# Seven block products in place of eight for the first matrix of each FFN, and the adaLN rows spread over both matrices

## Chip, cores and metric

One NeuronCore of a Trainium2 chip runs the whole program. The metric is the device time of one execution in microseconds; the kernel before has a median of 2449.19 us over 3 runs (2449.11 to 2454.41).

## The reference

Two sequences (128 context tokens, 512 sample tokens) go through two layers with shared weights. A layer has three sublayers: an FFN, a mixing block and a second FFN, each between a modulated norm and a gated residual.

```python
def modulate(h, mod, j):
    return h * (1 + mod[:, j + 1][:, None, :]) + mod[:, j][:, None, :]

def swiglu(h, w1, w2):
    g, u = jnp.split(h @ w1, 2, axis=-1)
    return (jax.nn.silu(g) * u) @ w2

def ffn_half(x, mod, j, g_pre, g_post, w1, w2):
    h = modulate(rms_norm(x, g_pre), mod, j)
    return x + 0.5 * mod[:, j + 2][:, None, :] * rms_norm(swiglu(h, w1, w2), g_post)
```

D_MODEL is 1024, D_FF 2816, everything in float32. The adaLN rows `mod` (nine vectors of 1024 per layer, for the sample and for the context) are products of a conditioning vector with w_mod (1024 x 9216 per layer).

## The kernel before

The 640 tokens are five tiles of 128: the A tiles 0 and 1 (256 columns), and the B tiles 2, 3 (sample) and 4 (context), 384 columns. A sublayer's input is kept transposed, features on partitions, as two float32r parts (hi and lo) of A (`h0hi`, `h0lo`) and of B (`h1hi`, `h1lo`). Every weight tile (128x512, 256 KB) is fetched by SP into one of five `raw` tiles, and split: ScalarE writes `whi` (L269), VectorE `wlo` = raw - whi (L271; GpSimd takes a share of these at stage starts). Eight split pairs are held, so weights are split up to five units ahead of use (`prefetch`, `unit`). A product is three float32r matmuls (L309): hi x hi, hi x lo, lo x hi.

An FFN sublayer (stages 0, 2, 3 and 5 of six) runs its first matrix in 22 slices f of 128 of d_ff. For each f the gate part and the up part are summed over eight k tiles: per f 4 weight tiles, 48 matmuls of A and 48 of B. For the first f of a stage (7, 5, 5, 7: `N_AONLY`) A runs alone while the boundary of the B tiles (residual, norm, modulation, transposes, splits: `bnd_steps`) is still being computed; these weights are then fetched once more for B alone; the rest run for A and B together. Then `act` = silu(gate) * up (L524, L534). The second matrix makes two passes over w2: `ffn2(l, i, 0)` for A, and `ffn2(l, i, 1)` for B beside A's boundary (`second_pass`).

The adaLN rows for later sublayers (`ada`) are made beside the f that run for A and B: VectorE accumulates 1024 columns over eight chunks for two sequences (16 instructions at L377 per row), TensorE reduces over partitions (L386), and the row is parked in DRAM. There are 16 such rows: 6 in stage 0, 6 in stage 2, 3 in stage 3 and 1 in stage 5. Matmuls and work beside them are interleaved by `run` with a rate; the tile framework then fixes each engine's order, and every engine works through its own order without overtaking, and so does SP's queue of transfers.

Of the kernel before, what the change touches and what calls it, by code (L numbers as in the profile page):

```python
# [15 lines left out]
P = 128  # L16
D = 1024
# [21 lines left out]
KEEP_F, KEEP_C = 2, 4  # L39
# [9 lines left out]
# schedule of each sublayer: skews between the tiles of a boundary, Pool share, matmul units ahead  # L49
# [92 lines left out]
class Builder:  # L142
    def __init__(self, ctx, tc, a, n_stage=6):
# [6 lines left out]
        self.rawp = pool("raw", 5)  # L150
        self.wp = pool("wsp", 8)
# [47 lines left out]
    def plan(self):  # L199
        a = self.a  # L200

        def ffn(l, i):
            def f1(f):
                for part in range(2):
                    for half in range(2):
                        c0 = part * FF + f * P
                        src = a["ffn_w1"][l, i, 512 * half:512 * half + 512, c0:c0 + P]
                        self.units.append((("w1", l, i, f, part, half), [(slice(0, P), src.rearrange("(k p) f -> p k f", p=P))]))
            na = N_AONLY[3 * l + 2 * i]
            for f in range(na):  # L210
                f1(f)
            for f in range(max(0, na - KEEP_F)):
                f1(f)
            for f in range(na, NF):
                f1(f)
# [30 lines left out]
    def _dma(self, i):  # L246
# [9 lines left out]

    def prefetch(self, upto):
        n = len(self.units)
        upto = min(upto, n - 1)
# [1002 lines left out]
```

## Time and profile before

| what | value |
|---|---|
| median of 3 runs | 2449.19 us |
| span of the profiled execution | 2446.1 us |
| lowest run, so what lies around the span | 2449.11 us, 3.0 us |
| TensorE busy | 2393.9 us, 98% |
| VectorE / ScalarE / GpSimd busy | 59% / 39% / 15% |
| DMA | 360.06 MB, mean 147 GB/s |

The page does not print the profiled execution's own device time; the span runs from its first to its last instruction. PE is TensorE, DVE VectorE, ACT ScalarE, POOL GpSimd, SP the queue that issues transfers. Consecutive instructions of an engine overlap at their ends, so the distance of two starts in a full queue is shorter than the duration of one.

### The profile page before, as it was taken

The page shows a single profiled execution, that of the slowest core. Times are in us where ns is not written, and L with a number is a line of the kernel's source. Part 1 is how long each engine was busy: PE and PEld are TensorE (multiplying, and loading weights), DVE is VectorE, ACT ScalarE, POOL GpSimd, SP SyncE. Part 2 cuts the span into 40 slices and gives each one's busy share as a digit, 9 for nine tenths or more (in the row PEclk, how much of TensorE's full clock was granted, in tenths as well). Part 3 has the DMA queues.
Part 4 walks back from the last instruction along what each step waited for, and adds up shares of the span by engine and source line. Part 5 has one row for each costly group of instructions (what it writes and reads, how often), then busy time and mean ns, then how long its engine had stood idle before and what let it go on. Part 6 is the DMA issues. An engine that isn't in the chain of part 4 may idle for free.

```text
span 2446.1 us, 37268 instructions
## 1 busy us (share of the span) xinstructions
PE 2393.9 (98%) x13892; PEld 2139.2 (87%) x13892; DVE 1444.2 (59%) x2162; ACT 956.4 (39%) x1982; POOL 365.9 (15%) x432
## 2 busy tenths in 40 slices
PE   8999999999999999999999999999998999999998
PEld 6999998877778999988889999988787899999887
DVE  6568766675776577746565642364758654422454
ACT  5422225455665222225443222354555553222443
POOL 2000000133434000001040000010634450000000
PEclk9999999999999999999999999999999999999999
DMA  9356655452235566635465632454522344422542
GB/s 295 111 179 228 213 189 165 146 171 89 65 104 151 162 215 219 192 122 165 137 181 155 197 110 75 129 168 130 159 86 82 116 143 139 140 76 74 166 154 90
DMA packets 332043, 360.06 MB, mean 147 GB/s; under 512 B 22019, under 2 KB 241411, under 8 KB 331862
## 3 DMA queue, kind: packets, MB, share of 16 engines
q1 hardware_dynamic: 328262, 344.59, 45.4%
q10 hardware_dynamic: 3600, 13.11, 1.4%
q8 instruction: 108, 1.77, 0.3%
q14 instruction: 73, 0.60, 0.1%
HBM read 341.50 MB, written 16.12 MB: 146 GB/s over the span
## 4 chain that ended last, share of the span: by engine, by line
PE 88%; DVE 4%; POOL 3%; issue 2%; ACT 1%; SPq 1%; DMA 0%; DVEq 0%; POOLq 0%; ACTq 0%
PE PS L309 85%; PE PS L386 1%; POOL tmp L459 1%; POOL wlo L271 1%; DVE ast L899 1%; PE PS L466 1%; PE PS L922 1%; DVE tl L305 1%; DVE wlo L271 0%; ACT pt L905 0%; DVE h1lo L305 0%; POOL r L316 0%; SPq L253 0%; PE PS L1042 0%; SPq L989 0%
## 5 line engine op out<-in xcount | busy, mean ns | idle before, releaser
L269 ACT ACTIVATE whi<-raw 128x512 fp32r<-128x512 f32 x864 | 541.3, 629 | 1093.4 <-PE PS L309 999.0
L271 DVE TENSOR_TENSOR wlo<-raw,whi 128x512 fp32r<-128x512 f32 x810 | 596.7, 740 | 580.0 <-ACT whi L269 555.5
L309 PE MATMUL PS<-h1hi,wlo 128*128 128x384 f32 (+1 forms) x1408 | 477.9, 339 | 0.0
L309 PE MATMUL PS<-h1lo,whi 128*128 128x384 f32 (+1 forms) x1408 | 477.0, 339 | 0.0
L309 PE MATMUL PS<-h1hi,whi 128*128 128x384 f32 (+1 forms) x1408 | 475.2, 337 | 0.0
L309 PE MATMUL PS<-h0hi,whi 128*128 128x256 f32 x1408 | 400.4, 285 | 8.3 <-DVE act L534 8.3
L309 PE MATMUL PS<-h0hi,wlo 128*128 128x256 f32 x1408 | 399.6, 285 | 0.0
L309 PE MATMUL PS<-h0lo,whi 128*128 128x256 f32 x1408 | 397.6, 283 | 0.0
L309 PE MATMUL PS<-whi,ahi 128*128 128x512 f32 x920 | 355.4, 394 | 0.0
L309 PE MATMUL PS<-wlo,ahi 128*128 128x512 f32 x880 | 348.3, 396 | 0.0
L309 PE MATMUL PS<-whi,alo 128*128 128x512 f32 x840 | 331.5, 397 | 0.0
L377 DVE SCALAR_TENSOR_TENSOR acc<-wmt,ccs,acc 128x1024 f32<-128x1024 f32 x224 | 278.4, 1281 | 26.9 <-DMA wmt<-in_w_mod 26.5
L309 PEld LDWEIGHTS PS<-h0hi,whi 128*128 128x128 f32 x1408 | 267.0, 190 | 26.5 <-issue 11.7
L309 PEld LDWEIGHTS PS<-h0hi,wlo 128*128 128x128 f32 x1408 | 266.3, 189 | 9.3 <-issue 8.4
L309 PEld LDWEIGHTS PS<-h0lo,whi 128*128 128x128 f32 x1408 | 267.4, 190 | 4.4 <-issue 4.2
L309 PEld LDWEIGHTS PS<-h1lo,whi 128*128 128x128 f32 x1408 | 265.2, 188 | 4.2 <-issue 4.2
L309 PEld LDWEIGHTS PS<-h1hi,wlo 128*128 128x128 f32 x1408 | 265.7, 189 | 1.7 <-issue 1.7
L309 PEld LDWEIGHTS PS<-h1hi,whi 128*128 128x128 f32 x1408 | 265.8, 189 | 0.0
L309 PEld LDWEIGHTS PS<-whi,ahi 128*128 128x128 f32 x920 | 173.6, 189 | 39.2
L315 POOL TENSOR_SCALAR v<-ss 128x1 f32<-128x1 f32 x60 | 24.6, 410 | 1175.4 <-ACT mk L437 1132.6
L309 PEld LDWEIGHTS PS<-wlo,ahi 128*128 128x128 f32 x880 | 166.0, 189 | 38.6
L309 PEld LDWEIGHTS PS<-whi,alo 128*128 128x128 f32 x840 | 158.6, 189 | 34.3
(200 smaller groups left out, 2722.1 us busy)
## 6 DMA issues: line engine op xcount, KB each, us to landing
raw<-in_ffn_w SPq DMA_DIRECT2D x736, 256.0 KB
wmt<-in_w_mod SPq DMA_DIRECT2D x136, 512.0 KB
raw<-in_w_in SPq DMA_DIRECT2D x80, 256.0 KB
xd<-x ACTq DMA_DIRECT2D x25, 512.0 KB
x<-xd SPq DMA_DIRECT2D x25, 512.0 KB
raw<-in_w_out SPq DMA_DIRECT2D x64, 128.0 KB
mdG<-rowG SPq DMA_DIRECT2D x12, 512.0 KB
mdS<-rowS SPq DMA_DIRECT2D x10, 512.0 KB
```

Of the source, the lines that this page charges most:

```text
L269: self.nc.scalar.activation(hi, r, AF.Copy)
L271: eng.tensor_tensor(lo, r, hi.bitcast(F32), ALU.subtract)
L305: i1 = (eng or self.nc.vector).tensor_tensor(lo, src, hi.bitcast(F32), ALU.subtract)
L309: self.nc.tensor.matmul(out, w, m, start=start, stop=stop)
L315: self.nc.gpsimd.tensor_scalar(v, ss, add, EPS, ALU.add, ALU.add)
L377: nc.vector.scalar_tensor_tensor(accs[s], w, self.cc[:, s, k:k + 1], prev, ALU.mult, ALU.add)
L386: nc.tensor.matmul(ps[32 * q:32 * q + 32, :], self.ones[:, 0:32], accs[q // 2][:, 512 * (q % 2):512 * (q % 2) + 512], start=True, stop=Tru ...
L459: nc.gpsimd.tensor_tensor(tmp[:, hs], tmp[:, hs], self.md["T", st][:, hs], ALU.add)
L466: nc.tensor.transpose(ps[:, P * k:P * k + P], tmp[:, 512 * h + P * k:512 * h + P * k + P], self.ident)
L899: nc.vector.tensor_reduce(mx, S, AX.X, ALU.max)
L922: nc.tensor.transpose(ps[:, w * c + P * j:w * c + P * j + P], pt[:, n * j + P * (c0 + c):n * j + P * (c0 + c) + P], self.ident)
```

## The change

Write X for one FFN's normed input, X1 for the A tiles and X2 for the two B tiles of x_sample, each cut into the two halves of its 1024 features, and B11, B21 (gate part, two halves of the features) and B12, B22 (up part) for the four weight tiles of an f. The four outputs (gate and up of X1 and of X2) are eight block products; Winograd's form of Strassen's scheme makes them from seven, of sums and differences of blocks. The context tile has no partner and keeps its four block products, which ride along as 128 more columns.

- First part (`ffn1_first`): for all 22 f, A times B11 and A times B21, 24 matmuls of 256 columns each f. The first product is copied into the B activation tile, their sum is A's gate.
- Second part (`ffn1_rest`): per f five products with the weights T2 = B22 - B11', B11' = B12 - B11, B22, B12' = B12 - B22 and B21' = B21 - T2, 12 matmuls each, one of 256 and four of 384 columns (386 in stage 0). Seven VectorE additions and two copies of ScalarE take them out of PSUM, then two silu and two products.
- The four subtractions of weight tiles (`combine`) are three on VectorE and the fourth, B12', on GpSimd. All four raw tiles of an f must be there; all blocks are fetched anew for the second part, so B11 and B21 come twice: 112 raw tiles more than before.
- The B boundary forms the differences of input blocks (`S1`, `SZ`, and B's first half replaced).
- Three adaLN rows of stage 0 and two of stage 2 run beside the second part, at a rate of 0.5; four in stage 0, four in stage 2 and three in stage 3 run beside the second matrix at 0.8; stage 5 has none.

```diff
-N_AONLY = (7, 0, 5, 5, 0, 7)
-ADA_RATE = 0.65
+ADA_ROWS = {0: (((0, "GST"),), ((1, "GST"), (2, "G"))), 2: (((2, "ST"),), ((3, "GST"), (4, "G"))), 3: ((), ((4, "ST"), (5, "G"))), 5: ((), ())}
+ADA_RATES = (0.5, 0.8)
+Q_POOL = (3,)
...
+            for f in range(NF):
+                for half in range(2):
+                    self.units.append((("w1", l, i, f, half), w1(l, i, f, 0, half)))
+            for f in range(NF):
+                for n, blk in enumerate((None, (0, 0), (1, 1), (1, 0), (0, 1))):
+                    self.units.append((("wq", l, i, f, n), w1(l, i, f, *blk) if blk else []))
...
+    def combine(self, i):
+
+        t2, b11, b22, b12, b21 = (self.raws[i + j] for j in range(5))
+        for j, (o, x, y) in enumerate(((b11, b12, b11), (t2, b22, b11), (b21, b21, t2), (b12, b12, b22))):
+            eng = self.nc.gpsimd if j in Q_POOL else self.nc.vector
+            eng.tensor_tensor(o, x, y, ALU.subtract)
...
+            m6 = yield from prod(0, SZ, 0, W, lo4)
+            nc.scalar.activation(yz, m6[:, WA:W], AF.Copy)
+            add(yx, m6[:, 0:WA], yx)
+            m5 = yield from prod(1, self.S1, 0, WA, lo4)
+            add(u[:, 0:WA], m5, yx)
+            m3 = yield from prod(2, SZ, WA, WA + W, lo4)
+            nc.scalar.activation(u[:, WA:W], m3[:, 0:zw], AF.Copy)
+            add(v, m3[:, zw:W], u[:, 0:WA])
+            m7 = yield from prod(3, h1, 0, W, lo4)
+            add(u, m7, u)
+            add(y, m7, y)
+            m4 = yield from prod(4, h1, 0, W, hi4)
+            add(y, m4, y)
...
+                self.rings(acc=(0, 1, 2, 3, 4, 5), ada=(6,))
+                bg = behind(tc, self.ada(rows[0], tile_of(self.tmpp, "wmt", "tmp"), tile_of(self.mdp, "acc", "mdS")), ADA_LAG)
+                run(self.ffn1_rest(l, i, late), (bg, ADA_RATES[0]))
...
+                bg = behind(tc, self.ada(rows[1], tile_of(wmp, "wmt"), tile_of(accsp, "acc")), ADA_LAG)
+                run(self.ffn2(l, i, 0), (bg, ADA_RATES[1]))
+                self.rings(ada=(7,))
+                self.second_pass(s, last, self.ffn2(l, i, 1, last), bg)
```

What this makes of the order is shown at three places. The first is VectorE in stage 3, one f that runs for all tokens. Before (f = 10; L534 makes `act`, L271 is a weight split, L377 an adaLN accumulation):

```order
L534 TENSOR_TENSOR act10_12295<-act10_12295,PS_79 128x256
L534 TENSOR_TENSOR act10_12296<-act10_12296,PS_79 128x384
L271 TENSOR_TENSOR wlo_14018<-raw_13878,whi_14017 128x512
L377 SCALAR_TENSOR_TENSOR acc0_13837<-wmt_13993,ccs_98,acc0_13837 128x1024
L377 SCALAR_TENSOR_TENSOR acc1_13838<-wmt_13993,ccs_98,acc1_13838 128x1024
L271 TENSOR_TENSOR wlo_14052<-raw_13912,whi_14051 128x512
```

and now, in the second part (f = 8; L281 is `combine`, L301 a split, L589 an evacuation or a product; raw_14873, 14920, 14940 and 14959 hold B11, B22, B12 and B21 of the next f, and the row behind the last one splits raw_14920, its B22):

```order
L281 TENSOR_TENSOR raw_14873<-raw_14940,raw_14873 128x512
L589 TENSOR_TENSOR uv_14915<-PS_79,act8_13078 128x256
L301 TENSOR_TENSOR wlo_14976<-raw_14853,whi_14975 128x512
L281 TENSOR_TENSOR t2_14995<-raw_14920,raw_14873 128x512
L589 TENSOR_TENSOR uv_14915<-PS_79,uv_14915 128x256
L281 TENSOR_TENSOR raw_14959<-raw_14959,t2_14995 128x512
L589 TENSOR_TENSOR act8_13054<-uv_14915,act8_13054 128x256
L301 TENSOR_TENSOR wlo_15001<-t2_14995,whi_15000 128x512
L589 TENSOR_TENSOR uv_14915<-PS_79,uv_14915 128x384
L589 TENSOR_TENSOR act8_13078<-PS_79,act8_13078 128x384
L301 TENSOR_TENSOR wlo_15023<-raw_14873,whi_15022 128x512
L589 TENSOR_TENSOR act8_13078<-PS_79,act8_13078 128x384
```

The accumulations are gone from this place, and subtractions, splits and evacuations alternate; an f has sixteen such rows.

The second place is SP's queue there, with what each transfer waits for. raw_15046, the B12 of the f after next, is the fifth transfer behind raw_14920 and takes its place in memory:

```order
L272 DMA raw_14920<-in_ffn_w1 128x4x128 [waits DMAHW6_49,DVE_49]
L272 DMA raw_14940<-in_ffn_w1 128x4x128 [waits DMAHW7_49,DVE_49,Pool_49]
L272 DMA raw_14959<-in_ffn_w1 128x4x128 [waits DMAHW0_49,DVE_49]
L272 DMA raw_14979<-in_ffn_w1 128x4x128 [waits DMAHW1_49,DVE_49]
L272 DMA raw_15026<-in_ffn_w1 128x4x128 [waits DMAHW2_49,DVE_49]
L272 DMA raw_15046<-in_ffn_w1 128x4x128 [waits DMAHW3_49,DVE_49,Pool_49]
```

Before, a transfer waited for one split; now the one for a B12 tile waits for VectorE and for GpSimd.

The third place is VectorE in stage 0's second part (f = 9 to 10; L408 is an accumulation, L624 A's last product):

```order
L408 SCALAR_TENSOR_TENSOR acc0_2446<-wmt_2448,ccs_98,wmt_2443 128x1024
L408 SCALAR_TENSOR_TENSOR acc1_2447<-wmt_2448,ccs_98,wmt_2443 128x1024
L589 TENSOR_TENSOR act10_934<-PS_79,act10_934 128x256
L281 TENSOR_TENSOR raw_2373<-raw_2463,raw_2373 128x512
L624 SCALAR_TENSOR_TENSOR act9_260<-uv_2425,act9_260 128x256
L589 TENSOR_TENSOR act9_895<-act9_895,uv_2425 128x384
L589 TENSOR_TENSOR uv_2549<-PS_79,act10_934 128x256
L281 TENSOR_TENSOR t2_2522<-raw_2430,raw_2373 128x512
L589 TENSOR_TENSOR uv_2549<-PS_79,uv_2549 128x256
L408 SCALAR_TENSOR_TENSOR acc0_2446<-wmt_2508,ccs_98,acc0_2446 128x1024
L408 SCALAR_TENSOR_TENSOR acc1_2447<-wmt_2508,ccs_98,acc1_2447 128x1024
L281 TENSOR_TENSOR raw_2483<-raw_2483,t2_2522 128x512
```

The 48 accumulations of three rows stand between the rows of the first 14 f here, 32 of two rows in the first 10 f of stage 2, and about 24 and 39 in the two passes of the second matrix of stages 0 and 2.

## Rows read from the trace of the kernel before

**Rows 1.** The page: span, busy time of TensorE and VectorE, chain by line

```profile
span 2446.1 us, 37268 instructions
...
PE 2393.9 (98%) x13892; PEld 2139.2 (87%) x13892; DVE 1444.2 (59%) x2162; ACT 956.4 (39%) x1982; POOL 365.9 (15%) x432
...
PE PS L309 85%; PE PS L386 1%; POOL tmp L459 1%; POOL wlo L271 1%; DVE ast L899 1%; PE PS L466 1%; PE PS L922 1%; DVE tl L305 1%; DVE wlo L271 0%; ACT pt L905 0%; DVE h1lo L305 0%; POOL r L316 0%; SPq L253 0%; PE PS L1042 0%; SPq L989 0%
```

**Rows 2.** Busy time by stretch; its columns stand in its first line

```profile
core 0: us, PE busy (x) PEld busy (x) DVE busy (x) ACT busy (x) POOL busy (x), PEclk, DMA share, GB/s
...
137.00:366.00 229.00, 229.00 (x1491) 214.72 (x1491) 169.14 (x192) 49.41 (x93) 4.77 (x5) 1.00 0.64 208
830.00:1087.00 257.00, 257.00 (x1680) 242.71 (x1680) 176.09 (x202) 55.59 (x105) 5.73 (x6) 1.00 0.60 192
1323.00:1572.00 249.00, 249.00 (x1659) 241.85 (x1658) 117.83 (x151) 54.71 (x104) 1.91 (x2) 1.00 0.42 132
2069.00:2284.00 215.00, 215.00 (x1451) 212.94 (x1450) 73.44 (x107) 48.33 (x91) 0.00 (x0) 1.00 0.35 108
...
82.00:137.00 55.00, 55.00 (x313) 55.00 (x311) 27.64 (x55) 24.31 (x44) 0.00 (x0) 1.00 0.43 123
750.00:790.00 40.00, 35.66 (x275) 33.89 (x274) 31.60 (x35) 21.55 (x47) 23.78 (x23) 1.00 0.48 145
366.00:430.00 64.00, 64.00 (x277) 51.95 (x276) 39.87 (x66) 34.29 (x69) 1.56 (x5) 1.00 0.53 162
430.00:523.00 93.00, 93.00 (x415) 76.36 (x414) 52.62 (x76) 43.25 (x82) 12.56 (x14) 1.00 0.47 143
```

**Rows 3.** Timeline of TensorE in stage 0, A and B together: start, duration

```profile
190.00 0.28 PE L309 MATMUL PS<-h0hi,wlo 128*128 128x256 f32 x1
190.12 0.34 PE L309 MATMUL PS<-h1hi,wlo 128*128 128x384 f32 x1
...
190.59 0.28 PE L309 MATMUL PS<-h0lo,whi 128*128 128x256 f32 x1
```

**Rows 4.** Groups of TensorE: count | busy us, mean ns | idle before

```profile
L386 PE MATMUL PS<-acc,ones 128*32 128x512 f32 x128 | 38.9, 605 | 0.0
```

**Rows 5.** Groups of VectorE, whole span

```profile
L271 DVE TENSOR_TENSOR wlo<-raw,whi 128x512 fp32r<-128x512 f32 x810 | 596.7, 740 | 580.0 <-ACT whi L269 555.5 <-PE PS L309 11.8 <-DMA raw<-in_ffn_w 2.9
L377 DVE SCALAR_TENSOR_TENSOR acc<-wmt,ccs,acc 128x1024 f32<-128x1024 f32 x224 | 278.4, 1281 | 26.9 <-DMA wmt<-in_w_mod 26.5
...
L534 DVE TENSOR_TENSOR act<-act,PS 128x384 f32<-128x384 f32 x88 | 48.4, 550 | 15.4 <-PE PS L309 15.4
...
L534 DVE TENSOR_TENSOR act<-act,PS 128x256 f32<-128x256 f32 x81 | 34.0, 419 | 99.3 <-PE PS L309 99.2
```

**Rows 6.** Timeline of VectorE, two of a kind in a row

```profile
84.61 1.28 DVE L271 TENSOR_TENSOR wlo<-raw,whi 128x512 fp32r<-128x512 f32 x2
...
220.09 2.48 DVE L377 SCALAR_TENSOR_TENSOR acc<-wmt,ccs,acc 128x1024 f32<-128x1024 f32 x2
```

**Rows 7.** Groups of VectorE from 1250 to 1280 us; timelines of GpSimd and VectorE

```profile
L271 DVE TENSOR_TENSOR wlo<-raw,whi 128x512 fp32r<-128x512 f32 x7 | 9.4, 1360 | 0.0
...
L305 DVE TENSOR_TENSOR h1lo<-PS,h1hi 128x512 fp32r<-128x512 f32 x6 | 4.1, 682 | 0.0
...
1243.91 1.30 POOL L271 TENSOR_TENSOR wlo<-raw,whi 128x512 fp32r<-128x512 f32 x1 [1.72 <-ACT whi L269]
...
1267.12 2.98 POOL L459 TENSOR_TENSOR tmp<-tmp,mdT 128x512 f32<-128x512 f32 x2 [2.39 <-DVE tmp L456]
...
1265.77 1.28 DVE L456 SCALAR_TENSOR_TENSOR tmp<-x,r,mdS 128x1024 f32<-128x1024 f32 x1
...
1267.56 1.39 DVE L271 TENSOR_TENSOR wlo<-raw,whi 128x512 fp32r<-128x512 f32 x1
```

**Rows 8.** Timelines of VectorE, SP and ScalarE around one weight tile

```profile
211.46 0.69 DVE L271 TENSOR_TENSOR wlo<-raw,whi 128x512 fp32r<-128x512 f32 x1
...
212.17 0.37 SPq L253 DMA_DIRECT2D raw<-in_ffn_w  x1
...
215.27 0.63 ACT L269 ACTIVATE whi<-raw 128x512 fp32r<-128x512 f32 x1 [4.11 <-DMA raw<-in_ffn_w]
```

**Rows 9.** Timelines of SP and ScalarE, a tile of w_in

```profile
541.34 2.81 SPq L253 DMA_DIRECT2D raw<-in_w_in  x3
...
544.12 0.63 ACT L269 ACTIVATE whi<-raw 128x512 fp32r<-128x512 f32 x1 [0.69 <-DMA raw<-in_w_in]
```

More of the change, by code (lines that the diff above doesn't have):

```diff
@@ L128, in run, with beside @@
                     break
+def beside(main, bg, rate):
+    due = 0.0
+    for ns in main:
+        due += ns * rate
+        while bg and due > 0:
+            try:
+                due -= next(bg)
+            except StopIteration:
+                bg = None
+        yield ns
+    if bg:
+        drain(bg)
 def drain(*gens):
@@ L200, in plan, with w1 @@
         a = self.a
+        def w1(l, i, f, part, half):
+            c0 = part * FF + f * P
+            src = a["ffn_w1"][l, i, 512 * half:512 * half + 512, c0:c0 + P]
+            return [(slice(0, P), src.rearrange("(k p) f -> p k f", p=P))]
         def ffn(l, i):
[L203 to L215, printed above, removed]
+            for f in range(NF):
[4 more added lines that the diff above has]
+                    self.units.append((("wq", l, i, f, n), w1(l, i, f, *blk) if blk else []))
             for g in range(2):
@@ L357, in rows, with ada @@
             r += [("S", n, l, 3 * sub + 1, 2 * sub, 1.0), ("T", n, l, 3 * sub, 0, 1.0)]
[L358 to L360 removed]
+        return [x for x in r if x[0] in kinds]
+    def ada(self, rows, wt, at):
         nc, a = self.nc, self.a
@@ L462, in bnd_steps @@
         hi, lo = self.hT[g]
+        four = lambda v: v.rearrange("p (k q) -> p k q", k=4)
+        blocks = t in GB and (s + (1 if post else 0)) % 3 != 1
         for h in range(2):
@@ new lines, in blocks, with new_s1, prod @@
+    def blocks(self, sp, late):
+        self.zw = P + 2 * late
+        self.SZ = [sp.tile([P, 4, 2 * WA + self.zw], F32R, name=f"sz{n}") for n in range(2)]
+    def new_s1(self):
+        self.S1 = [self.mdp.tile([P, D], F32, name=f"s1{n}", tag="mdG").bitcast(F32R).rearrange("p (k q) -> p k q", k=4) for n in range(2)]
+    def prod(self, out, w, m, cols, ks):
+        hi, lo = w
+        for j, k in enumerate(ks):
+            js = slice(P * j, P * j + P)
+            for q, (x, y) in enumerate(((hi, 0), (hi, 1), (lo, 0))):
+                self.mm(out, x[:, js], m[y][:, k, cols], j == 0 and q == 0, j == 3 and q == 2)
+            yield (cols.stop - cols.start) * 1.38
@@ new lines, in ffn1_first @@
+    def ffn1_first(self, l, i):
+        nc = self.nc
+        for f in range(NF):
+            pair = self.ps("acc")
+            for half in range(2):
+                w = self.unit(("w1", l, i, f, half))
+                yield from self.prod(pair[:, WA * half:WA * half + WA], w, self.hT[0], slice(0, WA), range(4 * half, 4 * half + 4))
+            if (f, 1) not in self.act:
+                self.act[f, 1] = self.ap.tile([P, WB + 2], F32, name=f"act{f}", tag=f"act1{f}")
+            y = self.act[f, 1][:, 0:WA]
+            nc.scalar.activation(y, pair[:, 0:WA], AF.Copy)
+            self.gate = nc.vector.tensor_tensor(self.act[f, 0], pair[:, WA:2 * WA], y, ALU.add)
@@ L1174, in second_pass @@
+    def second_pass(self, s, last, mm, bg=None):
         q = STG[s]
+        if bg:
+            mm = beside(mm, bg, ADA_RATES[1])
         b = self.boundary(s, GA, True, not last, 1, q["skew_a"])
```

238 lines of the change are left out of this document (125 added, 113 removed).

## Prediction

> **What bounds the kernel now.** I read the page first. TensorE is busy for 98% of the span, and 85% of the chain of waits that ended last is the one line that issues matrix products [rows 1]. VectorE has 59%, but that is a mean over stages, so the table by stretches comes next [rows 2]: while an FFN's first matrix runs for all tokens (the first four rows) TensorE never pauses, and VectorE is busy between 34% (73.4 of 215 us) and 74% (169.1 of 229 us), the more the more adaLN rows fall into the stretch. So fewer matrix columns are time won there, as long as VectorE keeps up. Third the timeline of TensorE [rows 3]: two pairs of a 256- and a 384-column product start within 0.59 us, so a pair costs 0.294 us. The products of 386 columns alone took 55 us for 313 [rows 2], 0.1757 us each; that leaves 0.119 us for 256 columns. One adaLN reduction is 38.9/16 = 2.4 us of TensorE [rows 4].
>
> Fourth, VectorE's prices [rows 5]: 0.69 us for 128x512 without disturbance [rows 8] (0.740 is the mean), 1.28 for an adaLN accumulation, 0.55 and 0.42 for 384 and 256 columns read from PSUM. They overlap when they queue: two 0.69 take 1.28, two 1.28 take 2.48 [rows 6]. So in a full queue I count 0.60, 1.19, 0.46 and 0.33 us.
>
> **The change part by part.**
>
> *TensorE.* Per f (one 128-wide slice of d_ff, 88 in all) there were 48 pairs, 48 x 0.294 = 14.11 us. Now 36 products have 256 columns and 48 have 384: 36 x 0.119 + 48 x 0.1757 = 12.72 us, of which 24 x 0.119 = 2.86 in the first part and 9.86 in the second. Saved: 1.39 x 88 = 122 us. The four stretches for all tokens held 64 f and all 16 reductions: 64 x 14.11 + 38.9 = 942 of their 950 us [rows 2]. The 8 us of small stalls go with them and I book them as won: 130 us together.
>
> *VectorE in the second part.* Per f it now has five splits and three subtractions of 128x512 (8 x 0.60), three evacuations of 256 and three of 384 columns (3 x 0.33 + 3 x 0.46), and two products of 256 and 384 columns, priced like the same widths from PSUM (0.33 + 0.46): 8.0 us, where it had 4 x 0.60 + 0.33 + 0.46 = 3.2. The new forms (128x386, SBUF to SBUF subtraction) lie between rows of the same width, so the bounds are narrow, 7.8 to 8.6. By itself 8.0 fits under TensorE's 9.86. Three things are added.
>
> First, GpSimd's subtraction, one per f. Undisturbed such an instruction takes 1.30 us [rows 7]. VectorE operations with two SBUF inputs stand still meanwhile: in the stretch where GpSimd was busiest the split took 1.36 us in the mean against 0.69, while the same width read from PSUM stayed at 0.68; the one at 1267.56 ended 0.53 us after the 1.30 of GpSimd's first operation from 1267.12 were over; and that operation had begun 0.07 us after VectorE released it [rows 7]. In the new order one PSUM read stands behind the operation that releases GpSimd, so 1.30 - 0.35 = 0.95 us of each is lost: 9.0 us per f. Ends: 0 and 1.30.
>
> Second, adaLN accumulations: 48 (three rows) within the first 14 f of the first FFN, 32 within the first 10 f of the second. VectorE needs 14 x 9.0 + 48 x 1.19 = 183 us there, TensorE 14 x 9.86 + 3 x 2.4 = 145; and 10 x 9.0 + 32 x 1.19 = 128 against 103. **Lost: 38 + 25 = 63 us** (ends: 39 without GpSimd's hold, 75 if each f with accumulations also waits 0.5 us for transfers).
>
> Third, a loop, in the 64 f without accumulations (8 + 12 + 22 + 22). There are five raw tiles and four are needed per f. The tile of B12 can only be fetched when the split of B22 of the f before has ended, and the first subtraction of the next f waits for B12. From the end of a split to the consumer of the next tile: split over at 212.15, issued 212.17, consumer starts 215.27: 3.12 us [rows 8]. From that subtraction to the end of the next B22 split the new order has: subtraction 0.69 and 0.07 to start GpSimd, its 1.30, the blocked split's last 0.47, then 4 x 0.60 (subtraction, subtraction, two splits), 2 x 0.33, 3 x 0.46 and a split of 0.69: 7.7 us. The loop is 10.8 us, TensorE's need 9.86; VectorE idles in it for 1.7 us with work behind the blocked subtraction. TensorE gets the T2 and B21 parts only 0.5 us ahead of its need, so the lead is gone after one f. **Lost: 64 x 0.94 - 2 = 58 us.** Ends: 0, where the lock costs nothing, and 1.3 us per f (83) with transfers slower by 0.4.
>
> The Trainium skill prices this transfer otherwise (DMA: Bandwidth & Descriptors, Anatomy of one DMA — SWDGE (gpsimd) path): 2.0 us fixed plus bytes over 436 GB/s, measured on another issuing path, an estimate of 2.6 us for 256 KB. By it the loop would be about 10.4 us, and the sum 26 us lower; by the row it stands.
>
> *The second matrix, first pass.* Three of the four FFNs now run 24 accumulations here, one and a half rows. TensorE needs 64 + 2.4 us [rows 2]. VectorE: 39.9 + 24 x 1.19 = 68. DMA: 53% of 64 us, plus 12 chunks of 0.5 MB (6.3 MB, at the 208 GB/s for 64% of the first stretch 19 us), plus x and G loads that moved here (2.6 MB, 8 us): 61 us. So about even: 3 us each, **8 us lost**, ends 0 and 30.
>
> *The first part.* The B boundary gets some 12 us more of VectorE work for two x_sample tiles (ten operations of 0.60 each), but 63 us instead of 28 to 40 to hide in. 0, ends -10 and +20. The 112 raw tiles more (29 MB) have one answer with the loop above: bandwidth is there (108 GB/s at 35% [rows 2]), the wait is what counts. ScalarE (five splits of 0.63 and four small ones, under 5 us per f) is covered.
>
> **Sum**, against the profiled execution: 2446.1 span and 3.1 around it (the median of the runs, 2449.2, is as much above the span): 2449.2 - 130 + 63 + 58 + 8 = **2448 us**. 0.3% (7 us) is about what a measurement of this kernel can tell from no change, so this case, 2430 to 2466 by itself, is no change or little either way.
>
> **The rivals.**
>
> *TensorE stays the bound.* GpSimd's hold falls into reads from PSUM and the wait for B12 hides behind it; then only the plain excess of accumulations is lost, 14 x 8.0 + 57 - 145 = 24 and 10 x 8.0 + 38 - 103 = 15. 2449.2 - 130 + 39 + 8 = 2366. For it: VectorE's plain 8.0 is 1.8 us below TensorE's need. Against it: the rows on the hold, and that the order of VectorE is fixed.
>
> *A shorter transfer.* A raw tile issued at 541.34 was consumed at 544.12 [rows 9], 2.78 us; the loop is then 10.5 and 64 x 0.3 = 20 us come back: 2428. The skill's figure above is of this kind. Against it: that tile comes from another matrix.
>
> *Slower: VectorE becomes the bound of the second matrix's second pass.* It has 52.6 of 93 us [rows 2]; 39 accumulations add 46, 99 us, where TensorE needs 93 + 3 x 2.4 = 100. Where VectorE was as full as its disturbances let it be, 31.6 of 40 us, TensorE lost 4.3 of 40 [rows 2], 11%. At that rate 100 us in three FFNs (the third with fewer) give 30 us: 2478. It decides as soon as accumulations stand ahead of a split in VectorE's queue. Against it: TensorE never paused in these passes so far, and weights are split ahead.
>
> That seven products are not what runs is excluded by the instruction list: TensorE's rows fall from 13,239 to 12,001.
>
> **How the numbers follow.** The sum 0.42, TensorE bound 0.22, shorter transfer 0.10, second pass 0.26. Faster by over 0.3%: 0.22 + 0.10 + a third of the sum's 0.42 = 0.46; within: 0.17; slower: 0.26 + 0.11 = 0.37. I predict the likeliest case. The range leaves out the far part of the first rival and the far part of the last: 2385 to 2486.
>
> **What would show it.** Right: in the two last FFNs' second parts the first subtraction (L281) waits for a DMA in nearly every f, and an f takes 10.5 to 11 us; in the first FFN's first 14 f VectorE is over 95% busy and an f takes about 13 us. VectorE's split beside GpSimd over 1 us. The second matrix keeps about 152 us. Wrong: an f of 9.9 us without accumulations (first rival); second-matrix stages of 165 us or more (last rival); TensorE idle at the change from first to second part by over 5 us, which I count at nothing.

## The result, and the profile after

The changed kernel takes 2547.7 us (median of 4 runs), the kernel before 2450.5 beside it: 1.040 times as long, 95% interval 1.0385 to 1.0415. The profiled span is 2546.3 us, 101 more than the sum of the prediction (2448 less the 3 us around the span).

The page of the changed kernel, answering to [rows 1, 5]; in the groups the count, then busy time, mean ns, and the idle time before them:

```profile
span 2546.3 us, 37919 instructions
...
PE 2350.9 (92%) x12836; PEld 2036.8 (80%) x12836; DVE 2065.5 (81%) x3279; ACT 1133.9 (45%) x2471; POOL 544.6 (21%) x549
...
PE 19%; DVE 12%; DMA 6%; issue 5%; POOL 2%; ACT 1%; DVEq 0%; SPq 0%; ACTq 0%; POOLq 0%
...
L301 DVE TENSOR_TENSOR wlo<-raw,whi 128x512 fp32r<-128x512 f32 x896 | 682.5, 775 | 137.2 <-ACT whi L299 132.3
...
L281 POOL TENSOR_TENSOR raw<-raw 128x512 f32<-128x512 f32 x88 | 122.8, 1395 | 908.8 <-DVE raw L281 560.0
...
L408 DVE SCALAR_TENSOR_TENSOR acc<-wmt,ccs,acc 128x1024 f32<-128x1024 f32 x224 | 296.0, 1345 | 18.7 <-DMA wmt<-in_w_mod 18.3
```

TensorE is busy for 43 us less (2350.9 against 2393.9) in a span 100 us longer, VectorE for 621 us more. The 43 us are not all that was saved: a product that starts behind a pause, or at half the granted clock, is shown as longer (in the last FFN's second part 1309 products are busy for 228 us, where the run dve4 below has 1312 in 214). Matmuls were 88% of the chain before; now the page follows the chain over 45% of the span only, and 19% are matmuls. Busy time by stretch, as in [rows 2]: the second parts of the four FFNs, the first part of stage 2, stage 0's second matrix by pass, and the last FFN's:

```profile
core 0: us, PE busy (x) PEld busy (x) DVE busy (x) ACT busy (x) POOL busy (x), PEclk, DMA share, GB/s
104.00:395.00 291.00, 252.98 (x1342) 231.96 (x1343) 258.47 (x402) 93.87 (x206) 35.25 (x24) 0.93 0.44 136
888.00:1152.00 264.00, 239.04 (x1325) 222.76 (x1324) 232.58 (x377) 83.84 (x184) 30.54 (x23) 0.95 0.43 129
1412.00:1654.00 242.00, 228.61 (x1314) 213.83 (x1313) 201.31 (x348) 81.17 (x183) 28.39 (x22) 1.00 0.34 97
2147.00:2390.00 243.00, 228.23 (x1309) 213.17 (x1309) 200.46 (x345) 80.56 (x182) 26.40 (x21) 1.00 0.33 97
806.00:887.00 81.00, 71.44 (x557) 69.56 (x556) 65.83 (x90) 52.66 (x111) 38.93 (x32) 0.96 0.52 154
395.00:465.00 70.00, 65.02 (x277) 49.74 (x276) 66.20 (x98) 31.81 (x64) 0.95 (x1) 1.00 0.91 306
465.00:573.00 108.00, 102.82 (x438) 78.41 (x437) 98.72 (x120) 47.29 (x91) 18.33 (x18) 0.97 0.67 217
2390.00:2450.00 60.00, 60.00 (x267) 49.74 (x266) 40.16 (x72) 32.00 (x65) 0.86 (x2) 1.00 0.68 222
2450.00:2540.00 90.00, 89.99 (x397) 74.17 (x396) 43.97 (x70) 35.20 (x68) 2.59 (x6) 1.00 0.36 119
```

With no rows beside it (the last FFN) a second matrix takes 60 + 90 us and TensorE never pauses; with four rows 70 + 108, and VectorE has 165 of the 178. Against the terms of the prediction (the stages' ends are read from TensorE's timeline):

| part of the four FFNs | by the sum | measured | more |
|---|---|---|---|
| first parts: products and transposes 274, and the 21 that TensorE already lost there before | 295 | 78.6 + 81.4 + 82.0 + 85.3 = 327 | 32 |
| second parts: 4 x 217 + 5 x 2.4 + 63 + 58 | 1001 | 291.3 + 265.1 + 242.2 + 243.4 = 1042 | 41 |
| second matrices: 4 x 154.4 + 11 x 2.4 + 8 | 652 | 178 + 177 + 171 + 150 = 676 | 24 |

That is 97 of the 101 us. The mixing stages lost 1 (by TensorE's timeline 232.1 and 236.1 us before, 232.9 and 236.4 now); the rest is in the rounding of the terms.

The loop of the raw tiles, in VectorE's, GpSimd's and SP's timelines of the last FFN's second part:

```profile
2303.87 0.69 DVE L281 TENSOR_TENSOR raw<-raw 128x512 f32<-128x512 f32 x1 [1.92 <-DMA raw<-in_ffn_w]
2304.48 0.42 DVE L589 TENSOR_TENSOR uv<-PS,act 128x256 f32<-128x256 f32 x1
2304.82 1.80 DVE L301 TENSOR_TENSOR wlo<-raw,whi 128x512 fp32r<-128x512 f32 x1
2306.55 0.68 DVE L281 TENSOR_TENSOR t<-raw 128x512 f32<-128x512 f32 x1
...
2311.02 0.67 DVE L301 TENSOR_TENSOR wlo<-raw,whi 128x512 fp32r<-128x512 f32 x1
...
2315.11 0.69 DVE L281 TENSOR_TENSOR raw<-raw 128x512 f32<-128x512 f32 x1 [1.82 <-DMA raw<-in_ffn_w]
```

```profile
2304.79 1.29 POOL L281 TENSOR_TENSOR raw<-raw 128x512 f32<-128x512 f32 x1 [10.05 <-DMA raw<-in_ffn_w]
```

```profile
2311.75 0.37 SPq L272 DMA_DIRECT2D raw<-in_ffn_w  x1
```

From the first subtraction to the end of B22's split 7.82 us (7.7 in the prediction), from there over the transfer to the next first subtraction 3.42 (3.12 predicted): 11.24 us per f. The split that meets GpSimd's 1.29 takes 1.80 in place of 0.69. The read from PSUM ahead of it lies beside GpSimd for its last 0.11 us only; one that lies wholly beside a subtraction of GpSimd, in stage 3, takes its 0.41 all the same:

```profile
1420.51 1.66 POOL L281 TENSOR_TENSOR raw<-raw 128x512 f32<-128x512 f32 x1 [7.45 <-DMA raw<-in_ffn_w]
...
1420.93 0.41 DVE L589 TENSOR_TENSOR uv<-PS,uv 128x256 f32<-128x256 f32 x1
```

### The profile page after: what moved, and what is told of

It is laid out like the page before. It is cut to its first block, busy times and chain, and to the rows that moved or that the text cites. A ratio compares the mean times of both kernels' runs of the same rounds, so it can differ in the third digit from the quotient of the medians.

```text
span 2546.3 us, 37919 instructions
## 1 busy us (share of the span) xinstructions
PE 2350.9 (92%) x12836; PEld 2036.8 (80%) x12836; DVE 2065.5 (81%) x3279; ACT 1133.9 (45%) x2471; POOL 544.6 (21%) x549
## 5 line engine op out<-in xcount | busy, mean ns | idle before, releaser
L301 DVE TENSOR_TENSOR wlo<-raw,whi 128x512 fp32r<-128x512 f32 x896 | 682.5, 775 | 137.2 <-ACT whi L299 132.3
L339 PE MATMUL PS<-sz,whi 128*128 128x384 f32 (+1 forms) x1408 | 381.7, 352 | 52.8 <-ACT whi L299 36.7
L281 POOL TENSOR_TENSOR raw<-raw 128x512 f32<-128x512 f32 x88 | 122.8, 1395 | 908.8 <-DVE raw L281 560.0
L339 PEld LDWEIGHTS PS<-sz,whi 128*128 128x128 f32 x1408 | 260.6, 196 | 69.4 <-ACT whi L299 44.6
L408 DVE SCALAR_TENSOR_TENSOR acc<-wmt,ccs,acc 128x1024 f32<-128x1024 f32 x224 | 296.0, 1345 | 18.7 <-DMA wmt<-in_w_mod 18.3
L339 PE MATMUL PS<-h1hi,whi 128*128 128x384 f32 (+1 forms) x704 | 249.9, 355 | 22.9 <-DVE uv L589 14.0
L339 PE MATMUL PS<-sz,wlo 128*128 128x384 f32 (+1 forms) x704 | 246.1, 350 | 12.4 <-DVE wlo L301 12.3
L339 PE MATMUL PS<-h1lo,whi 128*128 128x384 f32 (+1 forms) x704 | 240.2, 341 | 0.0
L339 PE MATMUL PS<-h1hi,wlo 128*128 128x384 f32 (+1 forms) x704 | 235.0, 338 | 0.0
L339 PE MATMUL PS<-h0hi,whi 128*128 128x256 f32 x704 | 206.1, 293 | 23.3 <-DVE act L585 22.9
L339 PE MATMUL PS<-h0hi,wlo 128*128 128x256 f32 x704 | 202.2, 288 | 1.2 <-DVE wlo L301 1.1
L339 PE MATMUL PS<-h0lo,whi 128*128 128x256 f32 x704 | 202.2, 287 | 0.0
L339 PEld LDWEIGHTS PS<-h1hi,whi 128*128 128x128 f32 x704 | 133.9, 190 | 52.3 <-DVE uv L589 24.5
```

The source lines that it names most:

```text
L281: eng.tensor_tensor(o, x, y, ALU.subtract)
L301: eng.tensor_tensor(lo, r, hi.bitcast(F32), ALU.subtract)
L339: self.nc.tensor.matmul(out, w, m, start=start, stop=stop)
L408: nc.vector.scalar_tensor_tensor(accs[s], w, self.cc[:, s, k:k + 1], prev, ALU.mult, ALU.add)
```

## The experiments

All times are medians of 4 to 10 runs with the kernel before beside them. Second parts and second matrices of stages 0, 2, 3 and 5, in us:

| run | median | ratio to before, 95% | second parts | second matrices |
|---|---|---|---|---|
| the change | 2547.7 | 1.0385 to 1.0415 | 291, 265, 242, 243 | 178, 177, 171, 150 |
| noada | 2435.1 | 0.9925 to 0.9957 | 248, 248, 241, 240 | 164, 164, 159, 150 |
| noacc | 2499.6 | 1.0186 to 1.0217 | 253, 243, 242, 240 | 191, 187, 166, 150 |
| dve4 | 2462.0 | 1.0029 to 1.0062 | 280, 253, 215, 214 | 176, 174, 169, 150 |
| dve4noada | 2345.7 | 0.9561 to 0.9593 | 232, 224, 215, 214 | 164, 163, 159, 150 |
| ring | 2532.4 | 1.0320 to 1.0352 | 268, 254, 252, 255 | 174, 174, 167, 150 |
| raw6 | 2522.4 | 1.0282 to 1.0312 | 270, 247, 228, 230 | 181, 182, 182, 154 |
| spread | 2460.4 | 1.0034 to 1.0064 | none | 171, 173, 161, 154 |
| nored | 2535.9 | 1.0339 to 1.0370 | 287, 270, 242, 241 | 173, 171, 171, 150 |
| rowsrate | 2503.1 | 1.0202 to 1.0236 | 282, 275, 231, 231 | 177, 170, 163, 150 |
| p1pool0 | 2530.5 | 1.0316 to 1.0354 | 290, 265, 241, 242 | 178, 176, 170, 150 |
| nosub | 2525.3 | 1.0288 to 1.0318 | 285, 264, 241, 242 | 177, 177, 171, 150 |
| p1act | 2540.1 | 1.0357 to 1.0388 | 293, 265, 240, 243 | 180, 176, 169, 150 |
| dve4p1 | 2451.2 | 0.9996 to 1.0022 | 281, 252, 214, 216 | 176, 174, 166, 150 |
| dve4raw6 | 2436.3 | 0.9925 to 0.9962 | 267, 239, 213, 213 | 176, 177, 172, 154 |
| rows6 | 2449.3 | 0.9989 to 1.0009 | 268, 239, 222, 222 | 177, 174, 169, 154 |
| best | 2436.4 | 0.9935 to 0.9964 | 269, 243, 228, 226 | 176, 173, 166, 154 |
| best2 | 2420.5 | 0.9871 to 0.9904 | 269, 246, 217, 217 | 176, 175, 170, 154 |

**Rows out, and GpSimd's subtraction moved: noada, dve4, and both.**

```diff
-            for k in range(KD):
+            for k in range(1):
```

> Leaves out 7 of the 8 steps of every adaLN row spread over the FFNs: 14 of 16 accumulations and 7 of 8 w_mod chunks of each of the 16 rows, so the rows are wrong; the reductions on TensorE stay. Theory (VectorE's accumulations and its fixed order set the first and third FFN): the second parts of the first two FFNs fall from 291 and 265 us to the 243 of the last two, the second matrices from 178, 177 and 171 us to about 152: 2547 - 48 - 22 - 26 - 25 - 19 = about 2407 us. The second parts of the last two FFNs stay at 242 to 244. Rival (the halved clock is a cost of its own, set by something else): the halved stretches stay, some 27, and the first FFN stays above 270 us in its second part.

```diff
-Q_POOL = (3,)
+Q_POOL = ()
```

> All four subtractions of blocks on VectorE, none on GpSimd. Theory (the subtraction on GpSimd costs more in VectorE's order than it takes off it): the loop over the raw tiles becomes 0.69 + 5 x 0.60 + 2.04 + 0.69 + 3.12 = 9.5 us, under TensorE's 9.86, so an f of the last two FFNs falls from 11.3 to 9.9-10.1 us, their second parts from 243 to about 220; in the first two VectorE needs 8.6 us per f instead of 9.0, second parts of about 278 and 247: total about 2547 - 2 x 23 - 13 - 18 = 2470 us. Rival (the hold by GpSimd costs nothing, VectorE's own work counts): 0.6 us more per f, 11.3 to 11.9 us, total 2547 to 2600.

> All four subtractions on VectorE, and 14 of 16 accumulations and 7 of 8 chunks of each adaLN row left out (the rows are wrong). Theory (besides hold and rows nothing stands in the way of TensorE in the second parts): second parts of 224, 220, 215 and 215 us, second matrices as in the run without rows, 164, 164, 159 and 150: total 2462 - 57 - 33 - 34 = about 2340 us. Rival (a sum of VectorE's work near 8.6 us per f already costs TensorE something each f): second parts of the first and third FFN 230 us or more, total 2360 or more.

Stretches of dve4 (second parts of stages 0 and 3) and of dve4noada (of stages 0 and 2), columns as above:

```profile
104.00:384.00 280.00, 252.36 (x1344) 232.72 (x1343) 255.80 (x429) 94.22 (x207) 2.87 (x3) 0.92 0.46 144
1384.00:1598.00 214.00, 214.00 (x1312) 214.00 (x1311) 194.02 (x370) 81.28 (x183) 0.95 (x1) 1.00 0.39 112
```

```profile
104.00:336.00 232.00, 227.70 (x1345) 219.74 (x1344) 204.76 (x387) 92.41 (x206) 2.87 (x3) 0.99 0.43 127
813.00:1036.00 223.00, 220.95 (x1329) 214.08 (x1328) 196.27 (x372) 81.80 (x184) 0.96 (x1) 1.00 0.42 121
```

The four kernels make a square: the rows (14 of 16 accumulations and 7 of 8 chunks of each) cost 113 us with GpSimd's subtraction and 116 without it, the subtraction costs 86 us with the rows and 89 without. So they are two separate causes, 202 us together; the sum of the prediction had 129 us for both (63, 58 and 8). Moving one instruction per f to the busier engine took 28 and 29 us off the last two second parts; TensorE then never pauses there. Without both the second parts take 885 us for 880 of products and reductions (232 for 224 in stage 0, 214 and 215 for 217 in the last two). noada's total missed by 28 us (2435 for 2407), as the expectation of 152 us for a second matrix left out the reductions, which stay: 154 and four of 2.4 make the 164. The clock's rival falls: the granted clock rises with the waits gone, 0.93 to 0.99 in stage 0.

**Accumulations out, chunks kept: noacc.**

```diff
-                for s in range(2):
+                for s in range(2 if k == 0 else 0):
```

> Leaves out the same 14 of 16 accumulations of each row (the rows are wrong), but keeps every transfer of the w_mod chunks. Theory (VectorE is what the rows cost): within 15 us of the run without both, some 2407 to 2422 us, second-matrix stages of 152 to 157 us. Rival (the transfers are what they cost, DMA is 83 to 88% busy in the first passes): the first passes of the second matrix stay at 67 to 70 us, the stages above 160, and the total above 2450.

In the second parts the question is answered: 253 and 243 us with the chunks, 248 and 248 without, so there VectorE's work is the price and not the transfers. In the second matrix the run answers it for the first pass alone. First and second pass of stage 0, and TensorE's longest wait in them:

```profile
357.00:422.00 65.00, 65.00 (x280) 49.68 (x280) 42.71 (x76) 31.66 (x61) 1.91 (x2) 1.00 0.96 348
422.00:548.00 126.00, 101.93 (x431) 78.98 (x430) 58.10 (x83) 44.98 (x88) 14.54 (x15) 0.88 0.51 172
```

```profile
PE PS L339 <- DVE wmt L426: 11.8, 1, 11.8
```

Without accumulations nothing paces the chunks; they crowd into the first pass (348 GB/s), where TensorE does not pause all the same: there too the accumulations were the price, and not the transfers. In the second pass TensorE then waits 8.0 us in one piece for a row's last accumulation and 11.8 for its evacuation. The total, 2500 us, lies where the rival had it, but for this reason, which neither theory had.

**The loop: ring and raw6.** A ring of two tiles for B12 alone; then six raw tiles for all.

```diff
+        t = (self.rawq if self.own(i) else self.rawp).tile([P, 512], F32, name="raw")
...
+            while self.n_dma < n and self.room(self.n_dma):
```

> The raw tile of B12 gets a ring of two tiles of its own beside the five, so that its transfer no longer waits for the split of the f before; nothing else changes. Theory (the loop through that tile sets an f at 11.3 us): an f without accumulations falls to what VectorE (9.0) or TensorE (9.86) needs, 9.9 to 10.1 us; second parts of the last two FFNs about 220, the 20 late f of the first two gain some 25 us: total about 2475 us. Rival (GpSimd's hold and VectorE's order set the f, the transfer is only late because VectorE is): the f stays above 11.0 us, total 2535 to 2550.

```diff
-RAWS, SPLITS = 5, 8
+RAWS, SPLITS = 6, 8
```

> Six raw tiles in place of five, so that the tile of B12 is fetched after the split of B11 (one split earlier); room for it comes from two chunk buffers in place of three beside the second matrix and five small statistic tiles in place of six. Theory (the loop through the raw tiles sets the f without accumulations): an f falls from 11.3 to about 10.6 us, the second parts of the last two FFNs from 243 to 228-232, total 2547 - 28 - 10 to + 10 (fewer chunk buffers) = 2505 to 2530 us. Rival (the run with a ring of its own for B12 brought nothing: GpSimd's hold and VectorE's fixed order set the f, a wait for a transfer only moves): second parts of the last two FFNs at 240 us or more, total 2540 to 2560.

With six tiles an f takes 10.8 us (10.6 expected) and the last two second parts 228 and 230: the theory, nearly to the number. The second matrices grew to 181, 182 and 182 us, with two chunk buffers in place of three; that part of the edit says nothing of the loop. With the ring they grew to 252 and 255 (2532 us in all, where the rival had 2535 to 2550), and the first subtraction still waits for a transfer, as do others (VectorE's waits in the last second part: total, times, longest):

```profile
DVE raw L287 <- DMA raw<-in_ffn_w: 52.5, 39, 2.2
DVE t L287 <- DMA raw<-in_ffn_w: 3.9, 7, 1.1
```

39 waits for 22 f: with a tile of its own for B12 the planned order has B21's subtraction some 6 us behind that of T2 (within 1 us in the change), and it waits for its own transfer there. The ring changed VectorE's order too, so it is no clean test; raw6 and dve4 carry the verdict.

**Rows beside the second matrix: spread and nored.** The kernel before with the rows dealt as in the change; the change without the reductions there.

```diff
+            run(self.ffn2(l, i, 0), (bg, ADA_RATE2))
+            self.rings(ada=(7,))
+            self.second_pass(s, last, self.ffn2(l, i, 1, last), bg)
```

> The kernel before, with the adaLN rows alone spread as the change spreads them (rows beside the second matrix too). Theory (the second matrix loses by the rows beside it, whatever the first matrix does): second-matrix stages of 172 to 178, 172 to 178 and 166 to 172 us where the kernel before has 154, with 11 rows of 2.4 us gone from the first matrix's stages: 2449 + 23 + 23 + 17 - 26 - 5 = about 2480 us. Rival (the second matrix is slower in the changed kernel for another reason of the change, the stream of weights): stages of at most 164 us (154 and four reductions), total within 6 us of 2449.

```diff
+            if self.nored:
...
+                    nc.sync.dma_start(dst[q // 2:q // 2 + 1, 512 * (q % 2):512 * (q % 2) + 512], accs[q // 2][32 * q:32 * q + 1, 512 * (q % 2):512 * (q % 2) + 512])
...
+                continue
```

> The changed kernel without the reduction over partitions and the norm weights of the 11 adaLN rows beside the second matrices (the rows are wrong); accumulations and chunks stay. Theory (VectorE's queue, full with accumulations, is what the second matrix loses by): only TensorE's own 2.4 us per row and a wait or two go, second-matrix stages of 165, 165 and 161 us, total 2547 - 35 = about 2512 us. Rival (TensorE's fixed order waits at each reduction for the last accumulation and for its bank): stages of 155 to 160 us, total 2500 or less.

Stage 0's second matrix in spread, and in nored:

```profile
359.00:530.00 171.00, 164.27 (x710) 127.12 (x709) 162.20 (x206) 77.40 (x148) 19.30 (x19) 0.99 0.72 241
```

```profile
391.00:564.00 173.00, 158.84 (x681) 125.04 (x681) 162.84 (x213) 76.67 (x149) 18.23 (x17) 1.00 0.74 252
```

Rows there lengthen the second matrix without Strassen's scheme too (171 for 154, at 95% of VectorE); of its 17, 19 and 7 us, 26 are the reductions that left the first matrix, and the total rose by 12 (31 were expected, and at most 6 by the rival). Taking 26 us of work off TensorE in nored won 12 us, between what the theory (35) and nothing would give; the rival's 155 to 160 us per second matrix did not come. VectorE, at 94%, is the bound, and TensorE's reductions mostly lie beside it.

**Rows dealt otherwise: rowsrate and rows6.** Both with all subtractions on VectorE; rows6 with dve4raw6's six raw tiles.

```diff
+ADA_ROWS = {0: (((0, "GST"),), ((1, "GST"),)), 2: (((2, "GST"),), ((3, "GST"),)), 3: (((4, "G"),), ((4, "ST"),)), 5: (((5, "G"),), ())}
+ADA_RATES = (0.32, 0.5)
```

> The changed kernel with all four subtractions on VectorE, and the adaLN rows dealt otherwise: three rows in each stage of the first and third FFN, one beside the fourth FFN's second part and one beside its second matrix, one beside the last FFN's second part, at slower rates (0.32 and 0.5), so that the accumulations lie among more f. Theory (VectorE's plain sum counts once nothing holds it): second part of the first FFN 22 x 8.6 + 48 x 1.19 = 246 us in place of 281, of the third 246 in place of 253, of the last two 217 to 220, the second matrices 166, 166 and 160: total 2462 - 35 - 7 + 5 - 25 = about 2400 us. Rival (a chunk that comes late stops VectorE's queue wherever it lies, and rates change nothing): within 15 us of the 2462 of the run with four subtractions on VectorE.

```diff
+ADA_ROWS = {0: (((0, "GST"),), ((1, "GST"), (2, "G"))), 2: (((2, "ST"),), ((3, "GST"),)), 3: (((4, "G"),), ((4, "ST"),)), 5: (((5, "G"),), ())}
```

> As the run with all splits and subtractions on VectorE and six raw tiles, with two adaLN rows moved: one from beside the third FFN's second matrix to beside the fourth's second part, one from beside the fourth's second matrix to beside the last FFN's second part. Theory (an accumulation costs nothing where the loop and VectorE leave 1.0 us per f free: 22 us for 16 accumulations of 1.19): the last two FFNs' second parts grow by 2 to 6 us only, where a row there cost 17 us with five raw tiles; the second matrices of the third and fourth FFN fall by 6 each: total 2436 - 5 = about 2431 us. Rival (an accumulation in VectorE's order costs its whole 1.19 us wherever it lies): second parts of the last two at 228 us or more, total 2448 or more.

Both theories failed, and rowsrate's rival as well (2503 us, 41 above dve4). One row cost 17 us beside a second part with five raw tiles and 8.5 with six, where VectorE is idle for some 25 us in all; beside a second matrix a row less won 7 us at most, and nothing in stage 0. A rate spreads a row only over the f in which it lasts (16 accumulations in 4 to 7 f), and in those f VectorE is over TensorE's 9.86 us; what idles behind them is no help. In stage 0, slower rates left the second part at 282 us: VectorE waits 9 us for chunks in dve4 there, and the sum of 246 us holds none of that; the rest of the gap wasn't traced.

**The first part: p1pool0, nosub, p1act.** Lost time here is a first part's length less its products at their spacing: 15, 16 and 18 us in stages 2, 3 and 5 of the change (before: 6, 7 and 7).

```diff
-                self.lo_pool = q["pool"]
+                self.lo_pool = 0
```

> The changed kernel, with every split of a weight on VectorE in the first part of the last three FFNs, where one in three or two went to GpSimd. Theory (GpSimd's splits hold VectorE's boundary work, and the two banks wait for VectorE): the first parts with the change to the second fall from 81, 82 and 85 us to about 76, total 2547 - 18 = about 2529 us. Rival (VectorE has simply too much to do beside the boundary of the B tiles): the first parts grow by 0 to 8 us each, total 2547 to 2571.

```diff
-        sub = lambda o, x, y, op=ALU.subtract: nc.vector.tensor_tensor(o, x, y, op)
+        sub = lambda o, x, y, op=None: None
```

> The changed kernel without the six subtractions and additions of 128x512 per x_sample tile at the boundary that feeds an FFN (the block differences are wrong). Theory (the added boundary work on VectorE is what the two banks of the first part wait for): TensorE's lost time in the first parts of the last three FFNs falls from 15, 16 and 18 us to 9 to 11 each, total 2547 - 18 = about 2529 us. Rival (the wait is for the boundary's older work and GpSimd's splits, which fell into other products before): within 6 us of 2547.

```diff
+            nc.scalar.activation(self.act[f, 0], pair[:, WA:2 * WA], AF.Copy)
-            self.gate = nc.vector.tensor_tensor(self.act[f, 0], pair[:, WA:2 * WA], y, ALU.add)
+            self.gate = nc.vector.tensor_tensor(self.act[f, 0], self.act[f, 0], y, ALU.add)
```

> The changed kernel with one addition more on ScalarE: in the first part it copies both products of a bank out, and VectorE adds them from SBUF, so that a bank no longer waits for VectorE. Theory (TensorE passes a bank every 2.9 us in the first part, where one f took 5.7 before, so a wait of 3 us in VectorE's queue now stops it): the waits of TensorE for the addition at line 585, 5 to 9 us per first part, go, the lost time of 15, 16 and 18 us falls to 6 to 8, total 2547 - 27 = about 2520 us. Rival (the first part waits for weights that VectorE splits, the bank is only where it shows): lost time within 3 us of before, total 2540 to 2550.

TensorE's waits in the first part of stage 2 (total, times, longest), in the change and in p1act:

```profile
PE PS L339 <- DVE act L585: 9.4, 6, 3.5
```

```profile
PE PS L339 <- ACT act L585: 11.8, 5, 5.4
```

Lost time became 14, 11 and 14 us without GpSimd's splits, 15, 12 and 14 without the subtractions, 16, 16 and 17 with the copies on ScalarE. So GpSimd's hold has 10 of the some 30 us that were added, the subtractions 8, and the totals came out as expected by 17 and 22 us only because other stages gained as well. In p1act the wait for the bank went to ScalarE, and time and lost time came out as its rival had them; the rival's reason, that TensorE really waits for weights, is not shown by it.

**Together: dve4p1, dve4raw6, best, best2.** dve4 with p1pool0; that with six raw tiles (and three `ahi` tiles, five small ones); that with the copies of p1act, in best with the rows of rows6, in best2 with the change's.

```diff
-Q_POOL = (3,)
-RAWS, SPLITS = 5, 8
+Q_POOL = ()
+RAWS, SPLITS = 6, 8
...
+                self.lo_pool = 0
...
+            nc.scalar.activation(self.act[f, 0], pair[:, WA:2 * WA], AF.Copy)
```

> Both: all four subtractions on VectorE, and every weight split of the first parts on VectorE. Theory (GpSimd's hold costs in both parts, and apart from each other): the gains add, 2462 - 17 = about 2445 us, level with the kernel before; second parts of the last two FFNs 214 to 216 us. Rival (the second parts only shift what the first parts gain): 2455 to 2465.

> As the run with all subtractions and all first-part splits on VectorE, with six raw tiles in place of five (room from three in place of four tiles of split activations, and five small statistic tiles in place of six). Theory (an accumulation costs its whole 1.19 us because it lengthens the loop from the split of a weight over the transfer to the next f, which has only 0.4 us to spare; a sixth raw tile gives it 1.0): second part of the first FFN 22 x 9.86 + 3 x 2.4 + 48 x 1.19 - 22 x 1.0 = 259 us in place of 281, of the third 238 in place of 253, the last two unchanged at 215: total about 2445 - 37 = 2408, up to 2435 if the second matrix loses by the fewer tiles. Rival (the chunk of w_mod that comes late stops VectorE's queue, whatever the raw tiles): second parts of at least 275 and 249 us, total 2440 or more.

> The kernel of the two rows moved, with the copies of the first part on ScalarE as well. Theory: the gains add, 2431 - 27 = about 2404 us. Rival (ScalarE, which splits the weights there too, becomes what the first part waits for): 2425 us or more.

> The run with all splits and subtractions on VectorE and six raw tiles, its rows where the change has them, with the second copy of the first part on ScalarE. Theory (moving the two rows cost 8.4 us each beside the second part and won 3 each beside the second matrix; the copies win 3 to 12 us per first part once no weight split waits for GpSimd and a sixth raw tile runs ahead): 2436 - 13 = about 2423 us, second parts of the last two FFNs 213 to 218 us, lost time in the first parts 11, 11 and 4 us. Rival (the copies helped only because the two rows lay elsewhere): 2433 us or more.

dve4p1 came to 2451 us (2445 expected), dve4raw6 to 2436 (2408, at most 2435), best2 to 2420 (2423). So the gains add, though less than expected where the rows lie: in dve4raw6 stage 0's second part stayed at 267 (259 expected). best failed (2436 for 2404): its first parts fell to 76, 76 and 69 us, but the last two second parts took 228 and 226 where rows6 has 222, which wasn't traced. Stage 3's second part and stage 5's first part in best2:

```profile
1353.00:1570.00 217.00, 217.00 (x1323) 217.00 (x1322) 192.99 (x373) 87.49 (x183) 0.96 (x1) 1.00 0.40 116
1973.00:2042.00 69.00, 66.95 (x555) 65.87 (x554) 66.51 (x105) 55.66 (x133) 17.46 (x16) 1.00 0.60 175
```

TensorE is without a pause in the one and loses 4 us in the other (10 and 11 in stages 2 and 3). best2 takes 0.989 of the kernel before, 28 us less; it computes what the change computes.

## Why the prediction was wrong

- **TensorE's saving (130 us): right.** Where nothing holds it (dve4noada) the second parts take 885 us for the 880 counted, and the page has 12,836 matmuls for 13,892, which is 12 fewer for each of the 88 f (the prediction's 13,239 and 12,001 stand in no trace).
- **The loop (58 us): right in its mechanism, small in size.** The first subtraction waits for a transfer in nearly every f and an f takes 11.2 to 11.4 us, where 10.8 was the sum: the transfer takes 3.42 us for 3.12. In two FFNs that is 5 us each. The hold is shown by dve4, the raw tiles by raw6. (The prediction's six additions out of PSUM per f are right; the section on the change says seven.) The Trainium skill (DMA: Bandwidth & Descriptors, Anatomy of one DMA — SWDGE (gpsimd) path) gave an estimate of 2.6 us; on SP's queue the trace has 3.36 from issue to consumer, and the measurement decides. With 2.6 us the prediction's own terms make a loop of 10.3 us and a sum 33 us lower, not 10.4 and 26. By the Trainium skill (SBUF — State Buffer, Who interferes with whom) a VectorE instruction with two SBUF inputs contends with a GpSimd instruction that reads SBUF, and one with at most one SBUF input, outside the 2-port modes, doesn't: the 1.80 and the 0.41 us above agree.
- **Accumulations beside the second part (63 us): the mechanism right, mis-sized.** "VectorE over 95% busy, an f about 13 us" failed: it is 88% busy in stage 0's rows, and an f takes 15.0. Its waits there come to 22 us, 11.5 of them for w_mod chunks (next fences: a stretch of stage 0's rows, and VectorE's longest waits from 104 to 320 us). Stage 0 is 22 us over the sum, as much as these waits, and stage 2 is 7 us over it. The upper bound of 75 had 12 us of this.

```profile
104.00:260.00 156.00, 130.49 (x657) 117.30 (x658) 137.58 (x206) 45.08 (x98) 18.00 (x12) 0.90 0.44 138
```

```profile
DVE acc L408 <- DMA wmt<-in_w_mod: 11.5, 13, 2.7
DVE raw L281 <- DMA raw<-in_ffn_w: 4.2, 2, 2.4
DVE act L589 <- ACT act L605: 3.2, 4, 1.1
DVE uv L589 <- PE PS L339: 2.2, 3, 1.1
```

- **The second matrix's first pass (8 us): the mechanism right, half the size.** By TensorE's timeline it takes 69.5, 68.2 and 68.9 us, where the 61.6 of the kernel before and one reduction make 64.0: 15 us. VectorE is busy for 66 of stage 0's 70 us, and noacc, which leaves the accumulations out and moves more data, takes 65.
- **The rival that VectorE bounds the second pass (30 us): it happened, beside the sum and not in its place.** The second matrices are 178, 177 and 171 us. Their second passes take 108.1, 108.9 and 102.5 us, where 92.8 and the reductions make 100.0, 100.0 and 97.6: 22 us. The sign, 165 us or more, could not tell this case from the sum, whose own terms give 167 for a stage with four rows (154.4, four reductions of 2.4, and 3); nor do they fit the "about 152" that was to show the sum right. In the table 7 of the 24 us are the first passes', and 22 less the 4 that the last FFN won are the second's. That the case was given 0.26 as an alternative to the sum is one failed step: nothing in its condition excluded the sum's own losses.
- **The first part ("0, ends -10 and +20"): failed, 32 us.** The cover named, 63 us in place of 28 to 40, was TensorE's time; what the boundary needs is VectorE's. In 81 us VectorE is busy for 66 beside GpSimd's 39, and two banks let TensorE run on for 5.7 us only (24 x 0.119 x 2). GpSimd's splits and the new subtractions account for 18 of some 30 us in runs that took each away alone; the rest is open (best2 cut it in stage 5, and leaves TensorE waiting for the boundary's additions on GpSimd in stages 2 and 3).
- **TensorE idle at the change of parts:** under 1 us, as counted.

Four of the five losses were named ahead of the run; what failed is that they were joined as alternatives, and that the first part's cover was counted on the wrong engine. The range ended 8 us above the dearest single case, at 2486, and the losses came together.

## What to carry to other kernels

Rivals that meet in different stretches add; only rivals for the same stretch exclude each other. When a change moves work from TensorE to VectorE, sum VectorE in every stretch that gets some of it, and add what its queue waits for. An instruction given to GpSimd to relieve VectorE can cost more than it takes off (86 us here for 88 subtractions of 0.60): count what it holds up on VectorE, and what loop it stands in.

## What was not expected of the hardware

TensorE's granted clock fell to half in short stretches where the waits were: its mean is 0.93 in stage 0's second part and 0.95 in stage 2's, against 1.00 in the last two, where TensorE also paused in every f, but for 0.6 us in the mean. One such stretch, in which TensorE did 22 products, and the 6.8 us ahead of it, in which it was busy for 3.9:

```profile
157.00:163.80 6.80, 3.90 (x18) 2.60 (x17) 6.63 (x11) 2.20 (x4) 2.80 (x2) 1.00 0.06 22
163.80:170.60 6.80, 6.11 (x22) 6.11 (x23) 4.87 (x10) 1.72 (x4) 0.00 (x0) 0.50 0.66 202
```

0.93 is some 41 us at 1.2 GHz out of 291. An estimate of the most that this can have cost is half of it, 20 us; but VectorE, the fuller engine there, waited only some 5 us for TensorE and ScalarE (3.2 and 2.2 in the fence on its waits). No run tried the clock alone, so its own price stays open. The second: the 660 products of the last second matrix take 149.8 us in the change and 154.2 in the kernel before, raw6, dve4raw6 and best2, with no wait in either (15.0 against 15.4 us for 66). In the change they start every 0.227 us in stages 2 and 3 as well, where the kernel before has 0.232: some 4 us were won there too, so the rows beside the second matrices cost that much more than the table shows. The kernels differ in how much memory their tiles take; why that should matter wasn't tried.
